# Attention norm: sums of squares ahead of the eighth input chunk's products, variance first on VectorE, the row's copies ahead of the next weights on ScalarE

## The chip, the cores and the metric

One core of one Trainium2 chip runs the whole program. The metric is device time in microseconds (us), the median of the runs shown: 1190.09 us before the change, from three runs between 1187.17 and 1190.45 us. One execution was taken with the hardware profiler; it took 1192.83 us, and its span, from the first instruction to the last, is 1191.1 us. All times of rows below count from the start of that span.

The engines are named as the profile names them: PE is TensorE (PEld its weight loads), DVE is VectorE, ACT is ScalarE, POOL is GpSimd, SP is SyncE, which here only issues transfers. A "q" behind a name (SPq, POOLq) is the engine's own queue of transfers.

## The reference, cut to what matters

Two decoder layers on 512 tokens of width 1024: attention, a feed-forward part (FFN), pooling, an FFN. Only the first norm and the attention's projections are touched by the change:

```python
y = xf * lax.rsqrt(jnp.mean(xf * xf, axis=-1, keepdims=True) + RMS_EPS)   # then * g
qkv = (h @ w_qkv)...reshape(B, S, N_ATTN_GROUPS, 3, HEADS_PER_GROUP, HEAD_DIM)
```

The mean of squares of each token scales that token's row. Since it is one factor per token, a product can be made with x * g first and be scaled by it afterwards. The kernel does so: it needs the 512 factors only when the first queries, keys and values leave their product.

## The kernel before, in words

Activations are held with the model width on the 128 partitions, in eight chunks of 128 x 512 tokens. Products run in a reduced-precision float format (fp32r). To keep float precision each operand is split in two: ACT writes a rounded copy ("hi", L91) and DVE the rest ("lo", L92), and PE does three matmuls in place of one: hi x hi, hi x lo, lo x hi (L324, L325, L327 in a plain product, L456 to L458 in the others, L933 in the first products). So every weight costs an ACT and a DVE instruction before PE may use it.

The start of the program goes like this. Five warm-up matmuls; then a loop over the eight input chunks (L912 to L935). For each chunk k, SP loads the chunk of x and the chunk of the first four weights, ACT and DVE split both, and PE adds 12 matmuls of 512 columns (three for each of four products: queries and keys of the first head, L933). ACT squares the chunk and DVE adds it to the running sum of squares (`square`, L375 to L380). Behind the loop stands `rstd` (L399 to L413): PE sums the squares over the partitions (L406, 16 small matmuls), DVE turns the sum into a variance (L409), POOL raises it to the power -0.5 in two halves (L412). `spread` (L415) multiplies that with the identity on PE, so that each of 512 columns of a PSUM tile holds its token's factor; ACT copies it out as `row` (L944) and copies one partition of it, reordered, as `line` (L946). PE turns `line` into columns with tiny matmuls (L950), and ACT writes the columns `rk`, with and without the score scale (L952, and L954 for the unreordered ones).

Two further plain products (the fifth and the sixth: 24 matmuls each) run around these steps. Behind them come products in a scheme that needs seven small products for eight (`seven`, L465), whose weights are made from four quarters: "b" takes two quarters as they are, "s" sums of quarters, "m" further sums, "l" a last quarter. For these, `Pair.load` (L165) brings quarters to the tiles `raw` and `rawhalf` by SP, and one more quarter is added onto `raw` in flight by a transfer of POOL's queue (L172); `more` (L186) adds the two `raw` tiles on DVE (L188, L189). The activations need sums as well: `prepare(k)` (L872), k from 0 to 3, has ACT scale two chunks into `room` (L576), DVE form differences and sums in `temp` (L582, L583, L587), and ACT and DVE split these into `near`, `t` or `tx`. After the first such product's "b" part come the first head's scores (L725, L745, L749), softmax, and `merge` (L777), which needs `far` from DVE (L765), which needs the scores' maxima and sums.

A planner in the code (`pump`) decides when the next weights are loaded and split. A scheduler then fixes, when the program is built, one order of instructions for each engine; each engine takes its instructions strictly in that order, and an instruction that waits holds all behind it on its engine.

Of the kernel before, what the change touches and what calls it, by code (L numbers as in the profile page):

```python
# [2 lines left out]

# [5 lines left out]
F32 = mybir.dt.float32  # L9
F32R = mybir.dt.float32r  # L10
AF = mybir.ActivationFunctionType
OP = mybir.AluOpType
# [3 lines left out]
P = 128  # L16
S = 512
D = 1024
KC = D // P
# [3 lines left out]
EPS = 1e-6  # L23
SCALE = 128 ** -0.5
NT = S // P
NI = P // NT
G = P + NI
Y16 = NT * NT
# [36 lines left out]
def trunk(ctx: ExitStack, tc: tile.TileContext, xT, xN, norms, w_first, w_qk, w_qkp, w_v0p, w_v12, w_out, w_outp, w_pair, w_down, w_dblock, w_pin, w_pgrp,  # L65
          consts, ident_in, invcnt_in, outT, outR):
    nc = tc.nc
# [19 lines left out]
    nc.vector.memset(nhalf, -0.5)  # L87
    nc.scalar.activation(ident[:, :1], ones, AF.Copy)

    def split(hi, lo, v):  # L90
        nc.scalar.activation(hi, v, AF.Copy)  # L91
        nc.vector.tensor_tensor(lo, v, hi.bitcast(F32), op=OP.subtract)  # L92

    def split_neg(hi, lo, v):
# [58 lines left out]
    class Pair:  # L153
# [21 lines left out]
        def take(self, name, ring, raw):  # L175
            self.w[name] = w = Held(ring, self.shift)
            w.n = self.n
            split(*(t[:, :raw.shape[-1]] for t in w.t), raw)

        def blocks(self):  # L180
            self.take("b", "w", self.a)
# [191 lines left out]
    acc = {}  # L373

    def square(layer, k, engine=None):  # L375
        sq = tmp.tile([P, S], F32, name="sq", bufs=3)
        nc.scalar.activation(sq, X[k], AF.Square)
        if layer in acc:
            (engine or nc.vector).tensor_add(sq, acc[layer], sq)
        acc[layer] = sq  # L380
# [15 lines left out]
            scaled(layer, k, t[:, 0], t[:, 1])  # L396
        square(layer, k)

    def rstd(parts):  # L399

        nt = parts[0].shape[1] // P
        pc = ps()
        for i, a in enumerate(parts):
            for t in range(nt):
                for c in range(0, P, NI):
                    nc.tensor.matmul(pc[c:c + NI, t:t + 1], a[:, t * P + c:t * P + c + NI], ones,  # L406
                                     start=i == t == 0, stop=i == len(parts) - 1 and t == nt - 1)
        v = tmp.tile([P, nt], F32, tag="var", name="var")
        nc.vector.tensor_scalar(v, pc[:, :nt], 1.0 / D, EPS, op0=OP.mult, op1=OP.add)  # L409
        r, n = tmp.tile([P, nt], F32, tag="rcol", name="rcol"), nt // 2  # L410
        for t in range(0, nt, n):
            nc.gpsimd.tensor_tensor(r[:, t:t + n], v[:, t:t + n], nhalf[:, :n], op=OP.pow)  # L412
        return [r[:, t:t + 1] for t in range(nt)]  # L413

    def spread(r):  # L415

        pr = ps()
        for t, c in enumerate(r):
            nc.tensor.matmul(pr[:, t * P:(t + 1) * P], c.to_broadcast([P, P]), ident,
                             start=True, stop=True)  # L420
        return pr
# [6 lines left out]
    def begin(n, layer, ks):  # L428
        return [Product(KC, stream(layer)).add(ks) for i in range(n)]
# [166 lines left out]
    def in_a_row(t):  # L596
        return t.rearrange("p (y x z) -> p x y z", y=Y16, z=2)


    with tc.tile_pool(name="opool", bufs=1) as opool:  # L600
        with tc.tile_pool(name="apool", bufs=1) as apool:
            const = apool.tile([P, 5 * P], F32, name="const")
            d0, d12, swap = const[:, :2 * G], (const[:, 2 * G:2 * G + P], const[:, 2 * G + P:3 * G]), const[:, 3 * G:3 * G + P]
            rows = {}
# [3 lines left out]
            def evac(h, u, p):  # L608
                g, c = QK[u]
                t = apool.tile([P, S], F32, name=f"qk{g}{c}")  # L610
                v = t if g else by_block(t)
                if c:
                    nc.vector.tensor_mul(v, p, rows["row"])
                else:
                    nc.scalar.copy(v, p if g else p.rearrange("p (y x z) -> p y x z", y=Y16, z=2))
                QKV[h, g, c] = t
# [255 lines left out]
            def prepare(k):  # L872

                h, t = normed(0, k, None, Room(), Temp())
                T["11", k] = halves_of(*U[k])[0]
                T["21", k], T["22", k] = halves_of(*U[k + K2])
                for i, names in enumerate((("1", "2"), ("3", "4"))):
                    if k < 2:
                        held["t", k, i], b = slot("t")
                        b = b[:, 0], b[:, 1]  # L880
                    else:
                        c = k - 2 + 2 * i
                        b = x_tile(c, "tx", F32R), x_tile(c + K2, "tx", F32R)
                    split(*b, t.t[:, i * S:(i + 1) * S])
                    for name, v in zip(names, halves_of(*b)):
                        T[name, k] = v
                t.done()
# [24 lines left out]
            for k in range(KC):  # L912
                if k % 2 == 0:
                    rawh, wh = Held("raw"), Held("w")
                    rawh.done()
                    wh.done()
                    raw, (hi, lo) = rawh.t, wh.t
                s = slice(k % 2 * NF * P, (k % 2 + 1) * NF * P)
                held["h", k], b = slot("h")
                U[k] = b[:, 0], b[:, 1]  # L920
                nc.sync.dma_start(X[k], xT[:, k, :])
                nc.sync.dma_start(raw[:, s], w_first[k])
                if k:
                    scaled(0, k, *U[k])
                    nc.scalar.activation(hi[:, s], raw[:, s], AF.Copy)
                else:
                    nc.scalar.activation(hi[:, s], raw[:, s], AF.Copy)
                    scaled(0, k, *U[k], on_dve=True)
                nc.vector.tensor_tensor(lo[:, s], raw[:, s], hi[:, s].bitcast(F32), op=OP.subtract)
                for j, (w, v) in enumerate(((hi, 0), (hi, 1), (lo, 0))):  # L930
                    for i, f in enumerate(lead):
                        c = (k % 2 * NF + i) * P
                        nc.tensor.matmul(f.p, w[:, c:c + P], U[k][v], start=k == j == 0, stop=k == KC - 1 and j == 2)  # L933
                if k:
                    square(0, k - 1)  # L935
            square(0, KC - 1)
            nc.sync.dma_start(ident, ident_in)
            nc.sync.dma_start(const[:, :3 * G + P], consts[:, :3 * G + P])
            rcol = rstd([acc[0]])
            prepare(0)  # L940
            lead += begin(1, 0, range(KC))
            rows["row"] = apool.tile([P, S], F32, tag="row", name="row")
            rk = apool.tile([P, NT, NT], F32, name="rk")
            nc.scalar.activation(rows["row"], spread(rcol), AF.Copy)  # L944
            line = scratch("line")
            nc.scalar.copy(line[:1].rearrange("p (x y z) -> p x y z", y=Y16, z=2), in_a_row(rows["row"][:1]))  # L946
            lead += begin(1, 0, range(6))
            p = ps()
            for b in range(NT):
                nc.tensor.matmul(p[:, b:b + 1], blk(line, b)[:1], ones[:1], start=True, stop=True)  # L950
            for i, scale in ((0, 1.0), (2, SCALE)):
                nc.scalar.activation(rk[:, i], p[:, :NT], AF.Copy, scale=scale)  # L952
                for t, c in enumerate(rcol):
                    nc.scalar.activation(rk[:, i + 1, t:t + 1], c, AF.Copy, scale=scale)  # L954
            lead[-1].add(range(6, KC))

            def later(f, *a):
                return lambda: f(*a)
# [14 lines left out]
            prepare(3)  # L973
            for u in range(NF, len(QK)):
                evac(0, u, lead[u].p)
            place = apool.tile([P, NT], F32, name="place")
            nc.sync.dma_start(place, consts[:, 3 * G + P:])
            for h in range(HEADS):
# [546 lines left out]
```

## Time and profile before

| What | Value |
|---|---|
| median of the three runs | 1190.09 us |
| the profiled execution's own time | 1192.83 us |
| its span | 1191.1 us |
| PE busy | 1177.6 us (99%) |
| DVE busy | 993.6 us (83%) |
| ACT busy | 752.8 us (63%) |
| POOL busy | 174.2 us (15%) |
| mean granted TensorE clock | 0.998 |

A row of the profile's timeline reads: start in us, duration in us, engine, line, operation, what is written <- what is read, size, count; in square brackets the idle time of the engine just before it, and what ended that time. Where several equal instructions follow each other they are one row. Durations overlap: the next instruction often starts some 0.1 us before the one ahead has ended, and matmuls even more so, so the distance of two starts counts where instructions stand back to back. A row by windows gives, for a stretch, each engine's busy time (and number of instructions), then the granted clock of TensorE, the transfers' share, and GB/s.

### The profile page before, as it was taken

What the parts mean: (1) busy time and instruction counts of PE and PEld (TensorE: products, weight loads), DVE (VectorE), ACT (ScalarE), POOL (GpSimd) and SP (SyncE); (2) the same over time, 40 slices, a digit from 0 to 9 for tenths busy, and PEclk for the clock granted to TensorE, in tenths of its full rate; (3) what the DMA queues carried; (4) which work ended last, traced back from release to release, by engine and by line L of the source; (5) the groups of instructions that cost most, each with busy time, mean ns of one, the idle gap of its engine ahead of it and who ended that gap; (6) DMA issues with size and microseconds to landing.
All of it is one profiled execution on the core that took longest, in us unless ns stands there. A gap on an engine that the chain in (4) does not pass through costs nothing.

```text
span 1191.1 us, 25533 instructions
## 1 busy us (share of the span) xinstructions
PE 1177.6 (99%) x10158; PEld 1124.8 (94%) x10158; DVE 993.6 (83%) x1747; ACT 752.8 (63%) x1349; POOL 174.2 (15%) x168
## 2 busy tenths in 40 slices
PE   9899999999999999999999999999999999999997
PEld 7799999999999999889999999988888999999997
DVE  7798888889789989698988997656879998898875
ACT  7675555647556568647756775685665775676553
POOL 1211211111121001311111111122130111111100
PEclk9999999999999999999999999999999999999999
DMA  8656666665766466967777777798685777777732
GB/s 261 161 141 169 175 153 160 169 166 129 189 168 158 140 190 165 251 132 181 191 194 196 191 190 193 201 269 209 129 187 109 195 195 192 203 195 189 198 93 72
DMA packets 85016, 209.95 MB, mean 176 GB/s; under 512 B 7952, under 2 KB 13216, under 8 KB 84896
## 3 DMA queue, kind: packets, MB, share of 16 engines
q1 hardware_dynamic: 53104, 145.63, 36.7%
q0 software_dynamic: 31504, 62.41, 31.6%
q8 instruction: 79, 1.29, 0.4%
q14 instruction: 41, 0.34, 0.1%
q10 hardware_dynamic: 288, 0.29, 0.1%
HBM read 206.19 MB, written 2.10 MB: 175 GB/s over the span
## 4 chain that ended last, share of the span: by engine, by line
PE 94%; ACT 2%; issue 1%; DMA 1%; DVE 0%; POOL 0%; SPq 0%; DVEq 0%; POOLq 0%; ACTq 0%
PE ps L456 21%; PE ps L458 21%; PE ps L457 21%; PE ps L324 6%; PE ps L325 6%; PE ps L327 6%; PE ps L849 2%; PE ps L632 2%; PE ps L634 2%; PE ps L633 2%; PE ps L725 1%; PE ps L745 1%; DMA x<-xT 1%; DMA raw<-w_v0p 1%; ACT w L91 0%
## 5 line engine op out<-in xcount | busy, mean ns | idle before, releaser
L91 ACT ACTIVATE w<-raw 128x1024 fp32r<-128x1024 f32 x271 | 286.6, 1062 | 160.9 <-PE ps L458 91.2
L92 DVE TENSOR_TENSOR w<-raw,w 128x1024 fp32r<-128x1024 f32 x271 | 330.7, 1222 | 55.3 <-ACT w L91 51.0
L456 PE MATMUL ps<-far,w 128*128 128x256 f32 x896 | 246.5, 275 | 0.0
L457 PE MATMUL ps<-far,w 128*128 128x256 f32 x896 | 246.5, 275 | 0.0
L458 PE MATMUL ps<-far,w 128*128 128x256 f32 x896 | 246.4, 275 | 0.0
L456 PE MATMUL ps<-near,w 128*128 128x256 f32 x749 | 211.2, 282 | 0.0
L457 PE MATMUL ps<-near,w 128*128 128x256 f32 x749 | 207.2, 277 | 0.0
L458 PE MATMUL ps<-near,w 128*128 128x256 f32 x749 | 207.2, 277 | 0.0
L456 PEld LDWEIGHTS ps<-far,w 128*128 128x128 f32 x896 | 168.2, 188 | 0.1
L457 PEld LDWEIGHTS ps<-far,w 128*128 128x128 f32 x896 | 168.2, 188 | 0.1
L458 PEld LDWEIGHTS ps<-far,w 128*128 128x128 f32 x896 | 168.2, 188 | 0.0
L456 PEld LDWEIGHTS ps<-near,w 128*128 128x128 f32 x749 | 141.1, 188 | 0.6
L457 PEld LDWEIGHTS ps<-near,w 128*128 128x128 f32 x749 | 141.2, 188 | 0.1
L458 PEld LDWEIGHTS ps<-near,w 128*128 128x128 f32 x749 | 141.1, 188 | 0.0
L324 PE MATMUL ps<-near,w 128*128 128x512 f32 (+1 forms) x332 | 126.2, 381 | 0.0
L327 PE MATMUL ps<-near,w 128*128 128x512 f32 (+1 forms) x332 | 125.5, 378 | 0.0
L325 PE MATMUL ps<-near,w 128*128 128x512 f32 (+1 forms) x332 | 125.3, 378 | 0.0
L172 POOL DMA_DIRECT2D raw<-w_pair x36 | 43.5, 1210 | 297.3 <-DMA raw<-w_pair 139.5
L327 PEld LDWEIGHTS ps<-near,w 128*128 128x128 f32 x332 | 62.5, 188 | 11.7
L324 PEld LDWEIGHTS ps<-near,w 128*128 128x128 f32 x332 | 62.4, 188 | 11.7 <-ACT near L91 0.4
L325 PEld LDWEIGHTS ps<-near,w 128*128 128x128 f32 x332 | 62.6, 189 | 11.3 <-DVE near L92 0.2
L188 DVE TENSOR_TENSOR raw<-raw 128x512 f32<-128x512 f32 x87 | 59.7, 686 | 6.4 <-issue 3.1
(339 smaller groups left out, 2736.4 us busy)
## 6 DMA issues: line engine op xcount, KB each, us to landing
raw<-w_pair SPq DMA_DIRECT2D x80, 512.0 KB, 5.0
raw<-w_qkp SPq DMA_DIRECT2D x42, 512.0 KB, 4.4
raw<-w_pair POOLq DMA_DIRECT2D x36, 512.0 KB, 7.6
raw<-w_dblock SPq DMA_DIRECT2D x32, 512.0 KB, 4.6
raw<-w_qkp POOLq DMA_DIRECT2D x21, 512.0 KB, 7.9
rawhalf<-w_pair SPq DMA_DIRECT2D x36, 256.0 KB, 5.2
raw<-w_v SPq DMA_DIRECT2D x16, 512.0 KB, 4.1
raw<-w_dblock POOLq DMA_DIRECT2D x16, 512.0 KB, 7.5
```

Of the source, the lines that this page charges most:

```text
L91: nc.scalar.activation(hi, v, AF.Copy)
L92: nc.vector.tensor_tensor(lo, v, hi.bitcast(F32), op=OP.subtract)
L172: nc.gpsimd.dma_start(self.b.rearrange("p (a c) -> p a c", a=2), self.src[:, None, 3 * n:].to_broadcast([P, 2, n]), accum_op=OP.add)
L188: nc.vector.tensor_add(a[:, :n], a[:, :n], b[:, :n])
L324: nc.tensor.matmul(self.p[:, cols], w[0][:, s], mh[:, cols], start=self.done == 0, stop=False)
L325: nc.tensor.matmul(self.p[:, cols], w[0][:, s], ml[:, cols], start=False, stop=False)
L327: nc.tensor.matmul(self.p[:, cols], w[1][:, s], mh[:, cols], start=False, stop=self.done == self.n)
L456: nc.tensor.matmul(dst, w.t[0][:, c], th, start=k == 0 and not on, stop=False, skip_group_check=on)
L457: nc.tensor.matmul(dst, w.t[0][:, c], tl, start=False, stop=False, skip_group_check=on)
L458: nc.tensor.matmul(dst, w.t[1][:, c], th, start=False, stop=k == n - 1, skip_group_check=on)
L632: nc.tensor.matmul(o, mh, wh, start=k == 0, stop=False)
L633: nc.tensor.matmul(o, mh, wl, start=False, stop=False)
```

## The change

The sums of squares are moved into the loop: `square` of chunk k - 1 now stands ahead of chunk k's products, and for the last chunk both squares, `rstd` and thus its 16 matmuls stand ahead of the 12 matmuls of that chunk. `rstd` writes into a column block of `rk` itself, and one POOL instruction makes the scaled block; the eight ACT copies of L954 are gone. The variance (L409) is given high priority. `prepare(0)` has its ACT instructions behind the last chunk's split. The fifth product starts with two of its eight chunks ahead of `spread`, the copies `row` and `line` are given high priority, and the sixth product's first four chunks (it was six) stand ahead of the tiny matmuls. From there to the end of the sixth product's copy out, the rounded copies of weights of the seven-product scheme (`pin`) keep the program's order on ACT.

```diff
-    def split(hi, lo, v):
-        nc.scalar.activation(hi, v, AF.Copy)
+    pinned = []
+
+    def split(hi, lo, v, pin=False):
+        made = nc.scalar.activation(hi, v, AF.Copy)
+        if pin:
+            tc.keep_in_program_order(made)
         nc.vector.tensor_tensor(lo, v, hi.bitcast(F32), op=OP.subtract)
...
-            split(*(t[:, :raw.shape[-1]] for t in w.t), raw)
+            split(*(t[:, :raw.shape[-1]] for t in w.t), raw, pin=bool(pinned))
...
-    def rstd(parts):
+    def rstd(parts, r=None):
...
-        nc.vector.tensor_scalar(v, pc[:, :nt], 1.0 / D, EPS, op0=OP.mult, op1=OP.add)
-        r, n = tmp.tile([P, nt], F32, tag="rcol", name="rcol"), nt // 2
+        with tc.high_priority() if r is not None else nullcontext():
+            nc.vector.tensor_scalar(v, pc[:, :nt], 1.0 / D, EPS, op0=OP.mult, op1=OP.add)
+        r, n = tmp.tile([P, nt], F32, tag="rcol", name="rcol") if r is None else r, nt // 2
...
+                if k:
+                    square(0, k - 1)
+                if k == KC - 1:
+                    square(0, k)
+                    rk = apool.tile([P, NT, NT], F32, name="rk")
+                    rcol = rstd([acc[0]], rk[:, 1])
+                    nc.gpsimd.tensor_scalar(rk[:, 3], rk[:, 1], SCALE, None, op0=OP.mult)
                 for j, (w, v) in enumerate(((hi, 0), (hi, 1), (lo, 0))):
...
-                if k:
-                    square(0, k - 1)
-            square(0, KC - 1)
             nc.sync.dma_start(ident, ident_in)
             nc.sync.dma_start(const[:, :3 * G + P], consts[:, :3 * G + P])
-            rcol = rstd([acc[0]])
-            prepare(0)
-            lead += begin(1, 0, range(KC))
             rows["row"] = apool.tile([P, S], F32, tag="row", name="row")
-            rk = apool.tile([P, NT, NT], F32, name="rk")
-            nc.scalar.activation(rows["row"], spread(rcol), AF.Copy)
             line = scratch("line")
-            nc.scalar.copy(line[:1].rearrange("p (x y z) -> p x y z", y=Y16, z=2), in_a_row(rows["row"][:1]))
-            lead += begin(1, 0, range(6))
+            with tc.issue_after(fore.ins):
+                prepare(0)
+            lead += begin(1, 0, range(2))
+            pr = spread(rcol)
+            with tc.high_priority():
+                nc.scalar.activation(rows["row"], pr, AF.Copy)
+                nc.scalar.copy(line[:1].rearrange("p (x y z) -> p x y z", y=Y16, z=2), in_a_row(rows["row"][:1]))
+            pinned.append(True)
+            lead[-1].add(range(2, KC))
+            lead += begin(1, 0, range(4))
...
-                for t, c in enumerate(rcol):
-                    nc.scalar.activation(rk[:, i + 1, t:t + 1], c, AF.Copy, scale=scale)
-            lead[-1].add(range(6, KC))
+            lead[-1].add(range(4, KC))
...
+            pinned.clear()
```

What this does to the built order is shown at three places. Line numbers of the changed kernel are larger than those of before by 2 (L91 is L93), 4 (L92 is L96, L188 is L192), 5 (L409 is L414, L583 is L588, L765 is L770) or more; the sections behind this one use the numbers of before.

**VectorE, from the second `prepare` on.** Before, where `var` is the variance and the row ahead of it is the "s" weights of the first values' product:

```order
L582 TENSOR_TENSOR temp<-room 128x2x256
L92 TENSOR_TENSOR w<-raw,w 128x1024
L92 TENSOR_TENSOR half<-rawhalf,half 128x512
L92 TENSOR_TENSOR w<-raw,w 128x1024
L409 TENSOR_SCALAR var<-ps 128x4
L188 TENSOR_TENSOR raw<-raw 128x512
L583 TENSOR_TENSOR temp<-temp,room 128x256
L189 TENSOR_TENSOR raw<-raw 128x512
L587 TENSOR_TENSOR temp<-temp,room 128x256
L92 TENSOR_TENSOR half<-rawhalf,half 128x512
```

And in the changed kernel, where the row of L192 is the first that needs the quarter added in flight:

```order
L587 TENSOR_TENSOR temp<-room 128x2x256
L414 TENSOR_SCALAR var<-ps 128x4
L96 TENSOR_TENSOR w<-raw,w 128x1024
L588 TENSOR_TENSOR temp<-temp,room 128x256
L192 TENSOR_TENSOR raw<-raw 128x512
L592 TENSOR_TENSOR temp<-temp,room 128x256
L193 TENSOR_TENSOR raw<-raw 128x512
L96 TENSOR_TENSOR near<-temp,near 128x512
L96 TENSOR_TENSOR t<-temp,t 128x512
L587 TENSOR_TENSOR temp<-room 128x2x256
L618 TENSOR_TENSOR qk_445<-ps,row 128x16x16x2
L618 TENSOR_TENSOR qk_449<-ps,row 128x512
```

The variance now stands ahead of three weight splits that stood before it, two of which moved far behind, and the two key copies (L618, which read `row`) moved ahead of the "s" and "m" weights.

**ScalarE, around the copies `row` and `line`.** Before:

```order
L954 ACTIVATE rk<-rcol 128x1 x8
L91 ACTIVATE half<-rawhalf 128x512
L91 ACTIVATE near<-temp 128x512
L91 ACTIVATE w<-raw 128x1024
L91 ACTIVATE t<-temp 128x512
L576 ACTIVATE room<-x,nrm 128x512 x2
L91 ACTIVATE w<-raw 128x1024
L944 ACTIVATE row<-ps 128x512
L91 ACTIVATE tx<-temp 128x512
L946 COPY line<-row 1x512
```

And in the changed kernel:

```order
L93 ACTIVATE near<-temp 128x512
L620 COPY qk_443<-ps 128x16x16x2
L93 ACTIVATE t<-temp 128x512
L620 COPY qk_447<-ps 128x512
L581 ACTIVATE room<-x,nrm 128x512 x2
L955 ACTIVATE row<-ps 128x512
L956 COPY line<-row 1x512
L93 ACTIVATE w<-raw 128x1024 x2
L93 ACTIVATE half<-rawhalf 128x512
L93 ACTIVATE tx<-temp 128x512
```

The eight small copies are gone, and the "s" and "m" weights of the values' product, which stood ahead of `row`, stand behind `line`.

**VectorE, at the last `prepare`.** Its sums `tx` are operands of the values' product. Before:

```order
L583 TENSOR_TENSOR temp<-temp,room 128x256
L613 TENSOR_TENSOR qk_488<-ps,row 128x512
L587 TENSOR_TENSOR temp<-temp,room 128x256
L92 TENSOR_TENSOR tx<-temp,tx 128x512
L92 TENSOR_TENSOR w<-raw,w 128x1024
L92 TENSOR_TENSOR tx<-temp,tx 128x512
```

And in the changed kernel:

```order
L588 TENSOR_TENSOR temp<-temp,room 128x256
L618 TENSOR_TENSOR qk_483<-ps,row 128x512
L96 TENSOR_TENSOR w<-raw,w 128x1024
L592 TENSOR_TENSOR temp<-temp,room 128x256
L96 TENSOR_TENSOR tx<-temp,tx 128x512
L733 SCALAR_TENSOR_TENSOR s_515<-ps,rk,b_508 128x160
L96 TENSOR_TENSOR tx<-temp,tx 128x512
```

A weight split of 1024 columns stands ahead of the first of the last two `tx`, where it stood between the two.

On the other engines: on PE the 16 small matmuls of the sums stand between the seventh and the eighth chunk's twelve, the spreading four stand behind 6 matmuls of the fifth product (they stood behind all 24), and the tiny ones behind 12 of the sixth (they stood behind 18). Further on, the matmul of `merge` (L777) comes four matmuls earlier and two of the eight transposes of values (L698) 26 matmuls earlier. On POOL the two powers stand ahead of the second transfer that adds in flight (they stood behind it). On SP the half-size load of the second query-key weights of the seven-product kind, which stood ahead of both full loads of these weights, stands behind them.

More of the change, by code (lines that the diff above doesn't have):

```diff
@@ L1 @@
 from collections import deque
-from contextlib import ExitStack
+from contextlib import ExitStack, nullcontext
 import concourse.bass as bass
@@ L924, in trunk @@
                     scaled(0, k, *U[k])
-                    nc.scalar.activation(hi[:, s], raw[:, s], AF.Copy)
+                    fore = nc.scalar.activation(hi[:, s], raw[:, s], AF.Copy)
                 else:
```

## The prediction

> **What bounds the kernel now.** The page's first part has PE busy nearly throughout, so only PE's few gaps can be won. I then read the list of waits for the first 120 us on PE:
>
> ```profile
> PE 1177.6 (99%) x10158; PEld 1124.8 (94%) x10158; DVE 993.6 (83%) x1747; ACT 752.8 (63%) x1349; POOL 174.2 (15%) x168
> ...
> PE ps L419 <- POOL rcol L412: 2.8, 2, 2.6
> PE ps L950 <- ACT line L946: 2.2, 1, 2.2
> ```
>
> These two waits are the ones that the change aims at: `spread` for the powers, the tiny matmuls for `line`. Together 5.0 us. The view by windows adds the clock behind the second one, and what the other engines do meanwhile:
>
> ```profile
> 42.80:46.20 3.40, 1.42 (x10) 1.36 (x11) 3.33 (x6) 3.40 (x7) 0.00 (x0) 1.00 0.92 170
> 46.20:49.60 3.40, 3.40 (x13) 2.93 (x12) 3.40 (x8) 1.93 (x5) 0.00 (x0) 0.50 0.54 135
> 39.00:56.00 17.00, 14.82 (x168) 13.15 (x167) 16.61 (x27) 11.76 (x20) 2.25 (x2) 0.90 0.47 117
> 56.00:65.00 9.00, 9.00 (x106) 8.68 (x105) 8.05 (x18) 6.19 (x20) 1.28 (x1) 1.00 0.57 127
> ```
>
> For 3.4 us PE ran at half clock: 1.7 us more. So PE alone promises 6.7 us. But the third row says that DVE was busy for 16.61 of 17 us in the same stretch: PE's gaps here lie beside an engine that has no gap. What PE wins must be matched by DVE, or PE waits for DVE a little later. So I follow DVE, back to where it last stood still, and forward to the next thing that PE needs from it:
>
> ```profile
> 22.67 1.38 POOL L172 DMA_DIRECT2D raw<-w_v0p  x1 [1.12 <-DVE sq L379]
> 33.23 1.06 ACT L91 ACTIVATE w<-raw 128x1024 fp32r<-128x1024 f32 x1 [5.45 <-issue]
> 34.32 1.23 DVE L92 TENSOR_TENSOR w<-raw,w 128x1024 fp32r<-128x1024 f32 x1 [5.03 <-ACT w L91]
> 35.47 0.16 DVE L409 TENSOR_SCALAR var<-ps 128x4 f32<-128x4 f32 x1
> 35.54 0.68 DVE L188 TENSOR_TENSOR raw<-raw 128x512 f32<-128x512 f32 x1
> 38.97 0.69 DVE L92 TENSOR_TENSOR half<-rawhalf,half 128x512 fp32r<-128x512 f32 x1 [1.48 <-ACT half L91]
> 40.45 1.22 DVE L92 TENSOR_TENSOR w<-raw,w 128x1024 fp32r<-128x1024 f32 x1 [0.18 <-ACT w L91]
> 57.09 1.26 DVE L752 SCALAR_TENSOR_TENSOR s<-ps,rk,b 128x160 f32<-128x160 f32 x4 [0.92 <-PE ps L749]
> 64.25 0.22 DVE L765 TENSOR_TENSOR far<-st,place 128x64 f32<-128x64 f32 x1
> 64.87 0.33 PE L777 MATMUL ps<-far,const 128*128 128x64 f32 x2
> ...
> raw<-w_qkp POOLq DMA_DIRECT2D x3, 512.0 KB, 7.6
> raw<-w_v0p POOLq DMA_DIRECT2D x1, 512.0 KB, 10.5
> ```
>
> The quarter that is added in flight onto the values' weights is issued at 22.67 and lands 10.5 us later, at 33.2. ACT's split and DVE's behind it stand waiting for it, and the variance, done on PE long before, stands behind them in DVE's order. That is why the powers are late. From 34.3 to L765 DVE has 2.6 us of gaps in 30 (1.48, 0.18, 0.92). `far` is out at 64.47, and PE takes it at 64.87 without a wait listed: PE and DVE arrive there 0.4 us apart. So a gain of PE alone is worth 0.4 us; the rest must come from DVE's chain, which starts when the transfer lands.
>
> **The change, part by part.** First PE up to the scores.
>
> ```profile
> 8.94 19.33 PE L933 MATMUL ps<-near,w 128*128 128x512 f32 x84 [0.57 <-ACT w L925]
> 26.86 0.69 DVE L582 TENSOR_TENSOR temp<-room 128x512 f32<-128x512 f32 x1
> 28.20 0.43 PE L406 MATMUL ps<-ones,sq 128*32 128x1 f32 x32
> 28.56 0.50 PE L324 MATMUL ps<-near,w 128*128 128x512 f32 x1
> 29.32 0.33 SPq L171 DMA_DIRECT2D rawhalf<-w_qkp  x1
> 34.20 1.06 ACT L615 COPY qk<-ps 128x512 f32<-128x512 f32 x2
> 35.71 2.00 POOL L412 TENSOR_TENSOR rcol<-var,nhalf 128x2 f32<-128x2 f32 x2 [2.25 <-DVE var L409]
> 36.87 0.71 PE L419 MATMUL ps<-ident,rcol 128*128 128x128 f32 x4 [2.56 <-POOL rcol L412]
> 40.84 1.32 ACT L576 ACTIVATE room<-x,nrm 128x512 f32<-128x512 f32 x2
> 43.01 0.57 ACT L944 ACTIVATE row<-ps 128x512 f32<-128x512 f32 x1
> 44.10 0.63 ACT L946 COPY line<-row 1x512 f32<-1x512 f32 x1
> 44.78 1.05 PE L950 MATMUL ps<-ones,line 1*128 1x1 f32 x8 [2.18 <-ACT line L946]
> 50.29 1.36 PE L725 MATMUL ps<-qk,qk 128*32 128x32 f32 x88
> 90.00:100.00 10.00, 10.00 (x90) 10.00 (x90) 7.70 (x11) 4.04 (x5) 1.23 (x1) 1.00 0.62 178
> ```
>
> A matmul of 512 columns takes 0.23 us (19.33 over 84), one of 256 columns 0.111 us (10.00 over 90). Sums ahead of the eighth chunk's 12: they start at 28.20 - 12 x 0.23 = 25.4. The variance follows DVE's L582, at 27.5; the two powers take 2.0 us, so they are out at 29.7. PE meanwhile ends the eighth chunk at 28.56, as before, and 6 matmuls of the fifth product at 29.9. The wait of 2.8 is gone. Spreading 1.2 (from 36.87, without the second wait of 0.2), then 18 and 12 matmuls (6.9): 38.0. ACT: the values' "b" split as before; `t` needs DVE's sums, which now stand behind the add that waits for the landing at 33.2, so it ends near 34.8 (0.6 for the add, 0.35 for a sum of 256 columns, 0.6 for `t` itself, all by the row of L188 and its length); one copy 0.5, two `room` 1.2, `row` 0.55, `line` 0.65: 37.7. The wait of 2.2 is gone too, with 0.3 us to spare. Tiny matmuls 1.0, 12 of the sixth product 2.8, 12 of 256 columns 1.3: the scores come at 43.1 in place of 50.29, and without a half clock ahead of them. The eight copies of L954 that go and the POOL instruction that comes I cost at nothing: ACT stands until 33.2 waiting for DVE's add either way, and POOL has nothing to do before its next transfer at 32; without that cover each is worth about 0.1 to 0.5. The pins only fix an order.
>
> So PE stands 7.2 us ahead at the scores. Now DVE, from the landing on:
>
> - Start: the first add behind the landing (L188) at 33.2 in place of 35.54, since ACT's and DVE's "s" splits no longer stand ahead of it: 2.34 us earlier. The landing itself I take as unchanged; of the transfers beside it only a half-size load moves (the one at 29.32, which now stands behind loads that wait for the landing).
> - Work up to L765, counted in the built orders: one 1024-column split more (1.15, from 34.32 to 35.47), one half split more (0.6, its 0.69 less the overlap), one raw add less (0.6), one L583 of 256 columns less (0.33, half of a raw add's time): 0.8 us more.
> - Gaps: 1.48 (behind the ACT copies) and 0.18 go; 0.92 goes, since the scores come earlier; new is one for `room`, which ACT ends at 36.5 while DVE is through with `t` at 35.7: 0.75. Together 1.83 us less.
>
> L765 thus comes 2.34 - 0.8 + 1.83 = 3.4 us earlier, at 60.9, and `far` is there at 61.1. PE takes it four matmuls earlier in its order, so the time to compare is 64.87 - 0.44 = 64.43. Gain there: 3.3 us. Where did PE's other 4 us go?
>
> ```profile
> 50.51 0.69 DVE L92 TENSOR_TENSOR tx<-temp,tx 128x512 fp32r<-128x512 f32 x1
> 54.09 0.28 PE L456 MATMUL ps<-tx,w 128*128 128x256 f32 x1
> 65.00:80.00 15.00, 14.86 (x131) 14.66 (x130) 13.80 (x32) 12.33 (x28) 3.58 (x4) 1.00 0.62 168
> 150.00:1191.00 1041.00, 1034.50 (x8799) 991.42 (x8797) 871.12 (x1531) 657.25 (x1155) 146.27 (x140) 1.00 0.69 176
> ```
>
> Into two new waits. One is at the last `tx`: 43.1 + 1.3 for the scores + 18 matmuls x 0.111 is 46.4. But up to the first `tx` of the last `prepare` DVE now has two 1024-column splits more (2.3), and one L583 less. It ended that `tx` at 51.2; now 51.2 - 2.34 + 2.3 - 0.33 - 0.9 of gaps is 49.9. The other is at L777: from this `tx` on PE had 10.8 us of work before (its matmuls started at 54.09), less 0.44 now, so it arrives at 60.2 and waits 0.9.
>
> From 65 to 80 PE was without a matmul for 0.14 us, at the transposes that now come earlier: about 0.1 more. From 150 on PE has 6.5 us without work, and no listed wait: what is won ahead is kept. Sum: 3.4 us. The profiled execution would take 1192.83 - 3.4 = 1189.4; it lies 2.74 above the median of the runs shown, so the forecast for the median is 1190.09 - 3.4 = **1186.7 us**.
>
> Bounds of what the rows don't show. The landing: the next transfers of this kind took 7.6, this one 10.5; between 0.5 later (should DVE's square that releases it come one instruction later) and 2.9 earlier; the gain moves one for one. DVE's new gaps: at best none (0.75 more), at worst the same 2.6 as before (1.8 less). Half clock: none, or 1.7 us on the path.
>
> **The clock.** In the row of 42.8 to 46.2 PE had 1.42 of 3.4 us of work, 1.05 of it the one-column matmuls of L950, and the next 3.4 us ran at half clock; the wait of 2.56 at 34 to 36.9 was followed by full clock. The Trainium skill (TensorE: Matmul & The Clock Gate, Part 1) says that the clock falls to half after an idle window of about 3.4 us, and that the windows run freely; here less than a whole idle window sufficed. By it the two waits at `tx`, some 3 us within 3.4, may well bring half clock again, at about 50 to 53; that costs 1.7 us, which would shorten the wait at L777 and so cost at most 0.8 of the sum.
>
> **The rivals.**
>
> - *The half clock falls behind the last wait.* If the windows lie so that the waits at `tx` are split and that at L777 (about 1 us) counts, PE loses 1.7 us where nothing hides it: a gain of 1.7, 1188.4. For it: the windows' phase is not fixed by the program. Against it: the first wait of 2.56 brought none. By the clock gate's rule this needs a whole idle window, which L777 alone does not give.
> - *The landing comes earlier* by up to 2.9: 3.4 + 2.9 = 6.3, 1183.8. For it: the 7.6 of its like. Against it: it is issued at the same time, beside the same loads but one.
> - *DVE keeps its old gaps* (ACT's pinned order makes DVE wait elsewhere): 3.4 - 1.8 = 1.6 or less, 1188.5 to 1190.
> - *Slower: the next transfer added in flight comes too late.* Its chain is released by the "s" split of the values' weights on DVE, which was done at 35.5 and is now done at about 40:
>
> ```profile
> 36.30 0.33 SPq L169 DMA_DIRECT2D raw<-w_qkp  x1
> 40.58 1.23 POOL L172 DMA_DIRECT2D raw<-w_qkp  x1 [2.86 <-ACT w L91]
> 60.53 1.06 ACT L91 ACTIVATE w<-raw 128x1024 fp32r<-128x1024 f32 x1 [1.62 <-PE ps L458]
> ```
>
>   So it is issued near 44 in place of 40.58 and lands near 52; the ACT split that reads it ran at 60.53, 3.4 us earlier is 57. It decides from a landing at 57 on, for ACT then holds the exponentials behind it, and PE the products; to eat all 3.4 it must land past 60.5, 16.5 us after its issue, where the longest here took 10.5. Each further us is a us slower: at 18 us 1191.6.
> - *The change does not do what it says*, if the powers still wait (POOL held): then PE waits at `spread`, but DVE's chain starts at 33.2 all the same; a gain near 3, no result of its own.
>
> **How the numbers follow.** Forecast 0.60 (1185.7 to 1187.8 with the smaller unknowns); DVE's gaps 0.11; late half clock 0.10; early landing 0.14; late transfer 0.05. The range that should hold 8 in 10 goes from the early landing, 1183.8, to DVE's old gaps, 1189.6. About 0.3%, 3.6 us, is what a measurement of this kernel can tell from no change. A gain of over 3.6 us: all of the early landing (0.14) and something under half of the forecast's 0.60 (0.27): 0.41. Slower by over 3.6 us: the late transfer's worst and what I overlook, 0.05. The rest, 0.54, is within 0.3%.
>
> **What would show it.** Right: no PE wait at `spread` or the tiny matmuls; the scores at about 43; PE waits of about 3 us at products on `tx` and 1 us at the matmul that is now L782, starting near 61; the first raw add right at the landing, and DVE with hardly a gap from there. Wrong: PE without waits at `tx` (DVE is not the bound, gain toward 7), a landing far from 33.2, or waits of PE behind 65 that were not there.

## The result, and the profile after

The change makes the kernel 0.3% faster. In the first comparison, 14 executions of each kernel, the median goes from 1189.32 us (1187.17 to 1191.88) to 1185.62 us (1185.20 to 1187.45); the ratio is 0.9972, with a 95% interval of 0.9963 to 0.9981. The prediction was 1186.7 against 1190.09, a ratio of 0.9971. So size and sign fit. But the profile after does not look as predicted, and its execution took 1185.55 us: 7.3 less than the profiled one of before, twice the gain of the medians. The list of waits of the changed kernel for TensorE's first 150 us, whole:

```profile
PE ps L916 <- DVE idle L913: 1.2, 1, 1.2
```

That is the wait at the very start, which both kernels have. The waits at `spread` and at the tiny matmuls are gone, as predicted; the new ones, at `tx` and at L782, are not there. The timeline of the changed kernel, for the steps of the prediction:

```profile
20.78 1.39 POOL L176 DMA_DIRECT2D raw<-w_v0p  x1 [0.98 <-DVE temp L587]
25.05 0.43 PE L410 MATMUL ps<-ones,sq 128*32 128x1 f32 x32
25.73 0.16 DVE L414 TENSOR_SCALAR var<-ps 128x4 f32<-128x4 f32 x1
25.98 2.30 POOL L417 TENSOR_TENSOR rk<-var,nhalf 128x2 f32<-128x2 f32 x2 [3.81 <-DVE var L414]
28.18 0.69 DVE L192 TENSOR_TENSOR raw<-raw 128x512 f32<-128x512 f32 x1 [0.83 <-DVE temp L588]
29.64 1.05 PE L424 MATMUL ps<-ident,rk 128*128 128x128 f32 x8
37.44 1.05 PE L962 MATMUL ps<-ones,line 1*128 1x1 f32 x8
42.77 1.36 PE L730 MATMUL ps<-qk,qk 128*32 128x32 f32 x88
56.31 0.21 DVE L770 TENSOR_TENSOR far<-st,place 128x64 f32<-128x64 f32 x1
57.02 0.33 PE L782 MATMUL ps<-far,const 128*128 128x64 f32 x2
```

PE's steps came where they were put: sums at 25.05 (forecast 25.4), tiny matmuls at 37.4 without a wait, scores at 42.77 (43.1). DVE's did not: the first raw add stands at 28.18 in place of 33.2. The reason is the landing, in the views of transfers and of windows of this execution:

```profile
raw<-w_v0p POOLq DMA_DIRECT2D x1, 512.0 KB, 7.3
39.00:56.00 17.00, 17.00 (x239) 16.10 (x237) 15.86 (x31) 9.62 (x25) 3.84 (x3) 1.00 0.73 174
```

The quarter was issued 1.9 us earlier than in the profile of before (20.78 against 22.67) and took 7.3 us in place of 10.5, so it landed at 28.1 and not at 33.2. With 5 us more in hand DVE is no longer the bound between 39 and 56: PE is busy for all 17.00 us, DVE for 15.86. The two profiles thus differ by the change and by the landing of one transfer. The runs had to separate the two.

### The profile page after: what moved, and what is told of

The parts are those of the page before. It is cut to its first block, busy times and chain, and to the rows that moved or that the text cites. A ratio compares the mean times of both kernels' runs of the same rounds, so it can differ in the third digit from the quotient of the medians.

```text
span 1183.7 us, 25523 instructions
## 1 busy us (share of the span) xinstructions
PE 1175.9 (99%) x10158; PEld 1124.1 (95%) x10158; DVE 992.8 (84%) x1747; ACT 751.8 (64%) x1341; POOL 173.7 (15%) x169
## 4 chain that ended last, share of the span: by engine, by line
PE 98%; issue 1%; ACT 0%; DVE 0%; POOL 0%; DVEq 0%; POOLq 0%; ACTq 0%
PE ps L461 21%; PE ps L463 21%; PE ps L462 21%; PE ps L328 7%; PE ps L331 7%; PE ps L329 7%; PE ps L854 2%; PE ps L637 2%; PE ps L639 2%; PE ps L638 2%; PE ps L945 2%; PE ps L730 1%; PE ps L750 1%; PE ps L916 0%; ACT w L93 0%
## 5 line engine op out<-in xcount | busy, mean ns | idle before, releaser
L93 ACT ACTIVATE w<-raw 128x1024 fp32r<-128x1024 f32 x271 | 286.5, 1062 | 157.0 <-PE ps L463 87.9
L96 DVE TENSOR_TENSOR w<-raw,w 128x1024 fp32r<-128x1024 f32 x271 | 330.4, 1221 | 51.0 <-ACT w L93 46.4
L192 DVE TENSOR_TENSOR raw<-raw 128x512 f32<-128x512 f32 x87 | 59.4, 682 | 7.5 <-issue 4.4
```

Of the source, the lines that this page charges most:

```text
L93: made = nc.scalar.activation(hi, v, AF.Copy)
L192: nc.vector.tensor_add(a[:, :n], a[:, :n], b[:, :n])
```

## The experiments

**Theories.** The *landing theory* is the prediction's: DVE's chain from the landing on sets the time, and what the change is worth depends on when the quarter lands. The *gap theory*, its rival: the two waits and the half clock of PE are the loss, wherever the quarter lands. All comparisons below are on the chip of the run, against the kernel before on the same chip.

**Both kernels again, unchanged.** Three more executions under the profiler: two of before, one of the change.

> The kernel before, unchanged, for a second profile. Chain theory (VectorE's work from the landing of the quarter added in flight sets the end): the profiled execution's time follows that landing, about 1191 to 1193 us with a landing near 33 us from the start of the span, about 1187 to 1188 with one at 30 or earlier. Gap theory (TensorE's two waits and the half clock are the loss, wherever the landing falls): the two waits of 2.8 and 2.2 are there at any landing, and executions near 1187 are those without half clock (1.7 us).

> The kernel before, unchanged, for a third profile. Landing theory: L777 starts at the landing plus 31.7 us (33.2 to 64.87, 30.4 to 62.1 in the two profiles so far) and the execution takes 1128 us more than that; an execution at the median of 1188.2 has L777 near 60.2 and its landing near 28.5.

> The changed kernel, unchanged, for a second profile. Chain theory: with a landing near 33 TensorE waits about 3 us in all at products on tx and 1 us at L782, and the execution takes 1187 to 1189; with a landing by 30 there is no such wait and it takes 1185.3. Gap theory: no waits and 1185 to 1186 at any landing.

Timed, the change has 1185.56 us (10 executions) against 1188.19 (32): a ratio of 0.9975, interval 0.9965 to 0.9984. By the medians the gain is 2.6 us; by the ratio, which goes by all executions and so by the late ones too, it is 3.0 us (1.9 to 4.2). The two unchanged copies of before have 1188.72 (ratio 1.0003) and 1188.22 (1.0002, against a median of 1188.17). The first repeat of before shows, in timeline, transfers and waits:

```profile
21.17 1.38 POOL L172 DMA_DIRECT2D raw<-w_v0p  x1 [0.62 <-DVE temp L582]
raw<-w_v0p POOLq DMA_DIRECT2D x1, 512.0 KB, 9.2
32.73 0.68 DVE L188 TENSOR_TENSOR raw<-raw 128x512 f32<-128x512 f32 x1
61.45 0.22 DVE L765 TENSOR_TENSOR far<-st,place 128x64 f32<-128x64 f32 x1
62.06 0.33 PE L777 MATMUL ps<-far,const 128*128 128x64 f32 x2
PE ps L950 <- ACT line L946: 2.2, 1, 2.2
PE ps L419 <- POOL rcol L412: 0.6, 2, 0.4
```

and the second repeat:

```profile
20.48 1.38 POOL L172 DMA_DIRECT2D raw<-w_v0p  x1 [0.71 <-DVE temp L582]
raw<-w_v0p POOLq DMA_DIRECT2D x1, 512.0 KB, 7.5
30.36 0.68 DVE L188 TENSOR_TENSOR raw<-raw 128x512 f32<-128x512 f32 x1
58.92 0.21 DVE L765 TENSOR_TENSOR far<-st,place 128x64 f32<-128x64 f32 x1
59.23 0.41 PE L777 MATMUL ps<-far,const 128*128 128x64 f32 x2 [0.79 <-PE ps L456]
```

The landing (issue plus flight) is at 33.2, 30.4 and 28.0 in the three executions of before. From L188 to L765 DVE takes 28.71, 28.72 and 28.56 us in them. This holds although PE's waits at `spread` are 2.8, 0.6 and none, those at the tiny matmuls 2.2, 2.2 and 0.6, and although the third has no half clock at all. What PE won there went into waiting for `far` (0.79 in the last row). The own times are 1192.83, 1190.03 and 1187.33; L777 started at 64.87, 62.06 and 59.23. The difference is 1127.96, 1127.97 and 1128.10: behind L777 all executions are alike. The first two, both with half clock, have landings 2.8 us apart and times 2.80 us apart. For before the landing theory holds, and the gap theory falls. The profile on which the prediction rested was a late landing: its execution lies above all but one of the 32 runs. The repeat of the change landed at 27.9 and has no wait either.

Whether the change itself moves the landing, two profiles of it cannot tell. The times give a rough estimate, with the rule that the table further down gives. By it a landing behind 30.4 gives over 1190.0 us in before and over 1185.95 in the change. In the two comparisons above these are 13 of 46 executions of before and 8 of 24 of the change: by this estimate late landings are about as frequent in both, and the gain is not one of earlier landings.

**The parts alone.** Sums, powers and variance in front (the `True` gives the variance its high priority), all else as before:

```diff
+                if k:
+                    square(0, k - 1)
+                if k == KC - 1:
+                    square(0, k)
+                    rcol = rstd([acc[0]], True)
                 for j, (w, v) in enumerate(((hi, 0), (hi, 1), (lo, 0))):
...
-            rcol = rstd([acc[0]])
```

> One part alone: sums and powers ahead of the eighth chunk, variance first; the row's copies, the product order and ScalarE's order as before. Gap theory: the wait of 2.8 at spread goes, the other stays: 2.5 to 3 us faster. Chain theory: the wait at spread goes, but the tiny matmuls then wait about 3 to 4 us instead of 2.2, since ScalarE's copy of the row still stands behind its weight splits, which wait for the landing; 1.4 to 2.4 us faster.

1186.39 us, ratio 0.9987 (0.9979 to 0.9996): 1.8 faster than 1188.19 by the medians, 1.5 by the ratio. In its profile the quarter landed at 28.5, PE did not wait at `spread` nor at the tiny matmuls, and 0.9 us at L778 (L777 of before), which started at 58.25. So the waits came out as neither theory had them, since both were computed for a landing at 33; the time lies within what the landing theory gave, 1.4 to 2.4 faster, and below the 2.5 to 3 of the gap theory.

The other part alone: row's copies, pinned order and order of the products as in the change, sums behind the eighth chunk, no priority for the variance.

```diff
+                if k:
+                    square(0, k - 1)
+            square(0, KC - 1)
...
+            rk = apool.tile([P, NT, NT], F32, name="rk")
+            rcol = rstd([acc[0]])
```

> The other part alone: the row's copies ahead of the next weights, the pinned order and the products' order of the change; sums behind the eighth chunk and the variance at its place in the order that the scheduler gives it, behind the two adds that wait for the landing. Gap theory: TensorE waits at spread for 4.5 to 6 us instead of 2.8, the wait at the tiny matmuls goes: within 1 us of before, or slower. Chain theory: in spite of the longer wait 1.5 to 2.7 us faster, since VectorE's adds stand right behind the landing.

1190.05 us, ratio 1.0013 (1.0001 to 1.0025): 1.9 slower, and here the landing theory, which gave 1.5 to 2.7 faster, is wrong. The gap theory had the time, though its wait of 4.5 to 6 us was 2.27. The rows of this kernel (timeline, then windows):

```profile
28.62 0.69 DVE L192 TENSOR_TENSOR raw<-raw 128x512 f32<-128x512 f32 x1 [1.09 <-issue]
30.17 0.15 DVE L414 TENSOR_SCALAR var<-ps 128x4 f32<-128x4 f32 x1
32.15 1.40 PE L424 MATMUL ps<-ident,rcol 128*128 128x128 f32 x8 [2.27 <-POOL rcol L417]
61.86 0.23 DVE L784 TENSOR_TENSOR far<-ps,place 128x64 f32<-128x64 f32 x1 [0.26 <-PE ps L782]
33.36:36.77 3.41, 3.41 (x11) 2.63 (x10) 2.15 (x4) 3.41 (x8) 0.00 (x0) 0.50 0.63 112
```

The variance stands behind the two adds that wait for the landing, PE waits 2.27 us for the powers and then runs 3.41 us at half clock (1.7 us lost): 4.0 us, and L782 starts at 61.49, 4.5 after that of the change. At L784 DVE waits for PE. With a landing at 28.1 and DVE's new order PE is the bound, and there its gaps count in full. Each theory is thus right on its own side of a border; the next runs place it.

**The landing moved.** First earlier: the quarter is written instead of added.

```diff
-   ...to_broadcast([P, 2, n]), accum_op=OP.add)
+   ...to_broadcast([P, 2, n]), **({"accum_op": OP.add} if added else added.append(n) or {}))
```

> The kernel before with the quarter of the first values' weights written instead of added (so these weights miss a sum); same size, same queue, same order of all instructions. Landing theory: the transfer takes 4 to 6 us in place of 7 to 10 and lands by 27, no instruction waits for it any more, and the time is that of the lowest executions of before, 1186.5 to 1187.5. Gap theory: the wait at the tiny matmuls and the half clock stay, 1188 to 1188.5.

> The changed kernel with the quarter written instead of added, same size, queue and order. Both theories: TensorE has no wait, 1185.0 to 1185.5, the bound set by TensorE's own work. Landing theory: the gain of the change is then only 1.5 to 2 us. Gap theory: it stays near 2.8.

The transfer takes 6.2 and 6.4 us now, and the landings are at 26.6 and 27.7. Before takes 1186.50 us (11 executions), the change 1185.72 (11): 0.8 us apart, less than either theory had it (1.5 to 2, and 2.8). The half clock is gone from before, of its waits 0.4 us at the tiny matmuls and 0.95 at L777 are left. The kernel before with adding has 1187.97 here, so writing alone brings before 1.5 of the 2.3 us that writing and the change bring together.

Then later, by an instruction on POOL ahead of the transfer (`late` is read by nothing; all other instructions keep their order):

```diff
+            added or added.append(nc.gpsimd.tensor_tensor(tmp.tile([P, 8], F32, tag="late", name="late"),
+                ones.to_broadcast([P, 8]), self.b[:, :8], op=OP.pow))
             nc.gpsimd.dma_start(self.b.rearrange("p (a c) -> p a c", a=2), ...
```

> The kernel before with one more POOL instruction (a power of 8 columns, into a tile that nothing reads) ahead of the transfer that adds the quarter onto the first values' weights; the order of all other instructions is unchanged. The transfer is issued about 4 us later. Landing theory: it lands near 34, the adds behind it, the scores and the matmul at L777 move with it: 3 to 4 us slower, 1191.5 to 1192.5. Gap theory: TensorE waits longer at spread, since the variance stands behind the landing, but not elsewhere; also slower by 3 to 4, with the waits of spread grown by that much and DVE's own gaps unchanged.

> The changed kernel with the same added instruction ahead of the same transfer, which then lands near 32, an us from the 33.2 of the prediction. Landing theory: TensorE waits some 2 us at products on tx and about 1 at L782, DVE has hardly a gap behind the landing and brings L770 at 59.5 to 60.5: 2.5 to 3.5 us slower than the changed kernel, 1188 to 1189, and still 3 to 4 faster than the kernel before with the same delay. Gap theory: nothing but DVE waits for the landing, TensorE has no new wait: 1185.3 to 1186.3.

The added instruction took 1.7 to 2.2 us, so the transfer was delayed by some 2 us and not by 4; it landed at 33.0 and 32.7. Both kernels became some 20 us slower than either theory had it, 1212.77 and 1209.71, but not at this place: L777 started at 64.3 and L782 at 59.8, and the loss came hundreds of us later (last section). So the pair was run again with a tile of other size, `tmp.tile([P, 32], ...)[:, :8]`.

> As the run with the delayed transfer in the kernel before, but the unused tile has 128 bytes in each of its two buffers in place of 32, so that the tiles placed behind it (far among them) move by 256 bytes and not by 64. Address theory (the 20 us that the delayed kernels lost behind the first 70 us came from products on far, whose rows went from 275 to 281-284 ns): they go, and the time is 1128 us plus the time of L777, near 1192. Delay theory (the delay itself costs them somewhere later): 1212 again.

> The same for the changed kernel. Address theory: 1188 to 1188.5 with a landing near 32.7, TensorE waiting 1.5 to 2 us at tx and 0.4 to 1 at L782; the change is then worth 3.5 to 4.2 us at this landing. Delay theory: 1209 again.

The medians are 1192.13 us for before (6 executions, 1190.28 to 1193.39) and 1188.99 for the change (12, 1186.51 to 1190.18), 3.1 apart; the 20 us are gone. The delayed kernel before, timeline:

```profile
22.34 1.39 POOL L172 DMA_DIRECT2D raw<-w_v0p  x1 [0.33 <-POOL late L172]
35.06 0.68 DVE L188 TENSOR_TENSOR raw<-raw 128x512 f32<-128x512 f32 x1
63.79 0.21 DVE L765 TENSOR_TENSOR far<-st,place 128x64 f32<-128x64 f32 x1
64.41 0.33 PE L777 MATMUL ps<-far,const 128*128 128x64 f32 x2
```

and the delayed changed kernel, timeline, transfers and windows:

```profile
22.52 1.40 POOL L176 DMA_DIRECT2D raw<-w_v0p  x1 [0.33 <-POOL late L176]
raw<-w_v0p POOLq DMA_DIRECT2D x1, 512.0 KB, 10.2
32.76 0.69 DVE L192 TENSOR_TENSOR raw<-raw 128x512 f32<-128x512 f32 x1 [5.61 <-issue]
36.19 0.69 DVE L587 TENSOR_TENSOR temp<-room 128x512 f32<-128x512 f32 x1 [0.60 <-ACT room L581]
42.78 1.36 PE L730 MATMUL ps<-qk,qk 128*32 128x32 f32 x88
48.85 0.39 PE L462 MATMUL ps<-tx,w 128*128 128x256 f32 x1 [1.62 <-DVE tx L96]
59.44 0.21 DVE L770 TENSOR_TENSOR far<-st,place 128x64 f32<-128x64 f32 x1
59.75 0.41 PE L782 MATMUL ps<-far,const 128*128 128x64 f32 x2 [0.38 <-PE ps L463]
39.00:56.00 17.00, 15.35 (x219) 14.02 (x218) 17.00 (x31) 12.01 (x26) 3.83 (x3) 1.00 0.67 176
```

This is the picture of the prediction, at a landing 0.5 us from its 33.2: the raw add right at the landing, one gap for `room` (0.60), scores at 42.78, PE waiting at `tx` and at L782, DVE busy for 17.00 of 17. The landing of the pair is the same (32.6 and 32.7), and the own times are 1192.26 and 1188.25: 4.0 us apart. The medians, 3.1 apart, are below the 3.5 to 4.2 that was expected; at which landings their executions ran is not known.

One run more, with 16 columns in place of 8:

> As the run before, with 16 columns in place of 8 in the added instruction, so that the transfer is issued 1 to 2 us later still. If VectorE's chain from the landing is the bound, the time grows by just what the landing grows, all of it in the waits at tx and L782: 1189.3 to 1190.3. If the time follows something else, it stays near 1188.3.

The transfer was issued 1.4 us later (23.89), but took 8.5 us, so that it landed at 32.4, 0.3 earlier than in the run before. L192 is at 32.46 (0.30 earlier), L770 at 59.15 (0.29), L782 at 59.47 (0.28), the own time is 1187.95 (0.30): the time follows the landing, not the issue. The median is 1189.10 (11 executions), against 1188.99. The 1189.3 to 1190.3 that was expected did not come, because issue and landing are not tied as assumed.

**The profiled executions of the two orders together**, without the pair that lost 20 us elsewhere (the landing is issue plus flight; own time less start of L777 is 1127.9 to 1128.1 for before, less L782 it is 1128.5 to 1128.6 for the change):

| kernel | landing | first raw add | L777 or L782 | own time |
|---|---|---|---|---|
| before, profile of the prediction | 33.2 | 35.54 | 64.87 | 1192.83 |
| before, delayed | 32.6 | 35.06 | 64.41 | 1192.26 |
| before, repeat 1 | 30.4 | 32.73 | 62.06 | 1190.03 |
| before, repeat 2 | 28.0 | 30.36 | 59.23 | 1187.33 |
| before, written | 26.6 | 28.98 | 58.54 | 1186.50 |
| change, delayed | 32.7 | 32.76 | 59.75 | 1188.25 |
| change, delayed further | 32.4 | 32.46 | 59.47 | 1187.95 |
| change, first profile | 28.1 | 28.18 | 57.02 | 1185.55 |
| change, repeat | 27.9 | 28.02 | 57.21 | 1185.70 |
| change, written | 27.7 | 28.39 | 57.14 | 1185.70 |

In before the time follows the landing one for one to within 0.5 us, over all landings from 28.0 to 33.2. In the change it does so when the landing is late (L782 27.05 us behind it), and stands at PE's own 57.1 when it is early: the border is a landing at 57.1 - 27.05 = 30.0, worked out from these rows; no profile of the change has a landing between 28.1 and 32.4. So by these rows the change is worth 4.0 us for landings from about 30 on, 1.8 for one at 28 (1187.33 against 1185.55), and 0.8 at 27. The gain of the medians, 2.6 (1188.2 and 1185.6), lies between: an execution of 1188.2 has its L777 at 60.2 and by these rows its landing near 28.6 to 29, an estimate. What is gained is also evenness: landings before 30 no longer show.

## Why the prediction was right, and where it was wrong

- **What bounds the kernel** was read rightly: not PE's waits of 5.0 us and half clock, but DVE's chain from the landing to `far`. All five profiles of before in which the quarter is added, delayed or not, have the same chain, 28.56 to 28.73 us from L188 to L765, with PE's waits and half clock coming and going (29.25 with the quarter written, where PE waits for DVE at L777). PE's own path is close behind, and it hangs on the same landing, since the variance and `row` stand behind it. In the three profiles with the half clock behind the tiny matmuls, the one of the prediction among them, PE reaches L777 0.3 us after it could have had `far`; in the two others it waits 0.79 for `far`.
- **PE up to the scores** came 0.3 to 0.6 us earlier than forecast at the sums, the tiny matmuls and the scores, at both landings. Only the powers were 1.4 us early (28.3 for 29.7), since DVE was earlier than in the profile of before; nothing waited for them.
- **The sum of 3.4** is about 0.6 too small for its own case, the late landing, where the pair shows 4.0. The start, 2.34 us earlier, holds: L188 stood 2.3 to 2.4 behind the landing, L192 at 0.1 behind it. The term that was mis-sized is the gaps. DVE between L188 and L765 of before, and between L192 and L770 of the delayed change:

```profile
35.54:64.25 28.71, 25.01 (x275) 22.72 (x276) 25.89 (x48) 19.50 (x49) 5.53 (x5) 0.94 0.56 134
```

```profile
32.76:59.44 26.68, 24.96 (x277) 22.20 (x275) 26.08 (x46) 19.83 (x43) 3.83 (x3) 1.00 0.65 154
```

  The chain is 2.0 shorter and not 1.0. The count of instructions was right (46 each; the 48 of before hold the ends of two earlier ones). Busy time grew by 0.2 only (25.89 to 26.08) and idle time fell by 2.2 (2.82 to 0.60), but busy time is not the measure here: an instruction that waits does not overlap the one ahead, so part of what a wait costs, about 0.1 us each, shows as busy time. By the distance of starts the work grew by the 0.8 that was forecast. The gaps were larger than the three that the prediction read off the list, as these rows of its profile show:

```profile
41.59 0.68 DVE L92 TENSOR_TENSOR t<-temp,t 128x512 fp32r<-128x512 f32 x1
42.38 0.69 DVE L582 TENSOR_TENSOR temp<-room 128x512 f32<-128x512 f32 x1
43.10 0.43 DVE L583 TENSOR_TENSOR temp<-temp,room 128x256 f32<-128x256 f32 x1
```

  Back to back an instruction of 512 columns takes 0.60 us from start to start (1.20 for the two `tx` that start at 46.24); here it is 0.79 and 0.72, and nothing is listed. Five such places hold 0.7 us in all, and the lost overlap at the three listed waits is 0.3 more. With the change they go.
- **Into two new waits**: right in place and kind, at the late landing only: 1.62 us at `tx` and 0.38 at L782, together 2.0 where 3 and 0.9 were forecast. DVE's chain came up to 1 us earlier than computed, and PE reached the awaited `tx` at 47.2 and not at 46.4, because four products on `tx` stand between it and the 18 that were counted.
- **"It lies 2.74 above the median"**: this step failed. The prediction carried the gain of the profiled execution over to the median, as if the 2.74 us were an offset of no matter to the change. They came with the late landing, the very thing that the gain depends on. At the median's landing PE is the bound after the change, and the gain of the medians is 2.6. The 3.4 was 0.6 too small for its own case, the case was too favourable by 1.4 for the median, and the median of before fell from 1190.09 to about 1188.2 with more executions. That the forecast ratio of 0.9971 lies so close to the measured 0.9972 and 0.9975 is therefore in part luck.
- **The rival "the landing comes earlier"** had its price wrong: 6.3, as if the landing came earlier in the changed kernel only. When both land early the gain shrinks, to 1.8 at 28. The 7.3 us between the two first profiles are the case it priced, and are not the gain.
- **The other rivals** did not come. No half clock fell in any of the six profiles of the changed kernel in its own order of instructions, also not behind the 1.62 us at `tx`. DVE did not keep its old gaps. The next transfer added in flight was issued at 39.29 with the early landing and at 44.16 with the late one (near 44 was forecast), and no PE wait shows behind L782.
- **What would show it wrong** was well chosen: "PE without waits at `tx`: DVE is not the bound" is what the profile after shows, and for that execution it is so.

## What to carry to other kernels

A profile is one execution. If the chain that sets the end starts at the landing of a transfer, look how far that execution lies from the median before carrying its numbers over, and work the gain out as a function of the landing: with two bounds that lie close, the gain of a change is the smaller of two sums, and which one holds changes from execution to execution. To place such a border, move the landing itself and leave the order of all instructions as it is.

## What was not expected

- **The landing of one 512 KB transfer** that adds in flight varied from 28.0 to 33.2 us with nothing changed: issue 20.48 to 22.67, flight 7.5, 9.2 and 10.5 us. Written instead of added it took 6.2 and 6.4. Part of the later issue in the first profile is a weight chunk at the start, for which ACT waited 1.44 us there and 0.20 in the first repeat. What sets the flight stays open.
- **Twenty us by 64 bytes.** The unused tile of 8 columns (32 bytes, two buffers) moved the tiles placed behind it by 64 bytes; that of 32 columns moved them by 256. Among these tiles is a large one which is also named `far` and is not the small one of L765. The groups of products on this `far`, from 529 us on, in the delayed kernel before with 64 bytes (line, tile, shape, count, busy us, mean ns of one):

```profile
L457 PE MATMUL ps<-far,w 128*128 128x256 f32 x896 | 254.8, 284 | 0.0
L456 PE MATMUL ps<-far,w 128*128 128x256 f32 x896 | 252.1, 281 | 0.0
L458 PE MATMUL ps<-far,w 128*128 128x256 f32 x896 | 251.4, 281 | 0.0
```

  and in the one with 256:

```profile
L456 PE MATMUL ps<-far,w 128*128 128x256 f32 x896 | 246.5, 275 | 0.0
L457 PE MATMUL ps<-far,w 128*128 128x256 f32 x896 | 246.4, 275 | 0.0
L458 PE MATMUL ps<-far,w 128*128 128x256 f32 x896 | 246.4, 275 | 0.0
```

  That is 758.3 against 739.3 us, 19 of the 20.6 us between the two delayed kernels of before (1212.77 and 1192.13). The products on `near`, a tile that did not move, kept their times (283 against 282 ns at L456, 277 against 276 at L457 and L458). That the address of the tile is the cause is what these two runs point to; which alignment it takes was not tried.
- **Half clock without an idle window.** The half clock came in stretches of 3.41 us. The delayed kernel before, by windows of that length, back from its half clock:

```profile
31.75:35.16 3.41, 1.84 (x9) 1.18 (x7) 1.31 (x3) 2.02 (x3) 0.00 (x0) 1.00 0.89 176
35.16:38.57 3.41, 1.99 (x12) 1.67 (x13) 1.93 (x5) 1.59 (x10) 2.00 (x2) 1.00 0.42 132
41.98:45.39 3.41, 1.20 (x10) 1.07 (x10) 3.34 (x6) 3.41 (x7) 0.00 (x0) 1.00 0.92 172
45.39:48.80 3.41, 3.41 (x11) 2.83 (x12) 3.41 (x7) 1.83 (x6) 0.00 (x0) 0.50 0.60 141
```

  A wait of 2.8 us, divided over the first two, left PE 1.84 and 1.99 us of work in them, and full clock followed; one of 2.2 within the third left 1.20, and half clock followed. In the first repeat of before it was 1.20 too, in the run with the row's part alone 1.21. In the delayed kernel before with 64 bytes it was 1.65, left by the wait at `spread`:

```profile
35.14:38.55 3.41, 1.65 (x10) 1.42 (x11) 2.20 (x6) 1.25 (x9) 2.00 (x2) 1.00 0.39 99
```

  In the profile of the prediction a window counted in the same way, from 32.54 to 35.95, held 1.76 us and was followed by full clock. So in these runs windows with up to 1.65 us of work brought half clock, and windows with 1.76 or more did not. The Trainium skill (TensorE: Matmul & The Clock Gate, Part 1) has free-running windows of about 3.4 us, with whose length this agrees, and names an idle window as the condition; here windows with 1.20 to 1.65 of 3.41 us of work were enough. In before the half clock behind the tiny matmuls cost about 0.5 us, as DVE was nearly the bound: from L188 to L777 it is 29.33 to 29.35 us in the three profiles with it, and 28.87 and 28.88 in the one without and the one where it fell earlier. In the run with the row's part alone it cost its full 1.7 us.
